# Hybrid attention and SSD backbone on one core: low passes of the value product one key block later, the context rows' norm in nine steps, a modulation with one pass less

## The chip, the cores and the metric

The kernel runs on one core of one Trainium2 chip. The metric is the device time of one execution in microseconds (us). TensorE is called PE, its weight loads PEld, VectorE DVE, ScalarE ACT, GpSimd POOL, and SyncE, which issues most transfers, SP. Each engine works through its own instructions in a fixed order and waits for the others by semaphores. The transfers that an engine issues stand in that same order.

## The reference

The kernel computes a two-layer network for 1024 latent rows and 256 context rows with a model width of 1024. Layer 0 is windowed attention (16 query heads, 4 key heads, blocks of 128 rows; each block sees its neighbours and the context), layer 1 a bidirectional state-space mixer (SSD). The parts that the change touches are these:

```python
for i in range(DEPTH):
    shift, scale, gate = adaln(c, w_ada[i], b_ada[i])          # likewise *_c for the context
    u = rms_normalize(h) * (1.0 + scale[:, None]) + shift[:, None]
    uc = rms_normalize(hc) * (1.0 + scale_c) + shift_c
    y, yc = attention_mixer(u, uc, ...) if i % 2 == 0 else ssd_mixer(u, uc, ...)
    h = h + gate[:, None] * y
    if i < DEPTH - 1:
        hc = hc + gate_c * yc

# in attention_mixer, for a block of queries
s = jnp.einsum('bqkgd,bskd->bkgqs', qb, kb).astype(jnp.float32) * scale
p = sink_softmax(s, sink_kg, mask).astype(vb.dtype)
o = jnp.einsum('bkgqs,bskd->bqkgd', p, vb)
y_lat = ((o * jax.nn.silu(g)) @ w_out).astype(h_lat.dtype)
```

## The kernel before

**Numbers in two halves.** A float32 operand is split into a high part (a cast on ACT) and a low part (operand minus high part), and a product is three passes on PE: high by high, low by high, high by low (L236 to L238 for the projections). The names ending in H and L, or h and l, are these parts: `uH` and `uL` of the normed rows, `wh` and `wl` of the weights (L222 cast, L224 subtraction on POOL), `ph` and `pl` of the transposed softmax weights.

**Tiles.** The rows are held in three tiles, 0 and 1 with 512 latent rows each and 2 with the 256 context rows, transposed, so that a tile is eight slabs of 128 columns of the model by its rows. A norm (`rstd_n`, from L357) sums squares over partitions with PE (L354), takes the root on ACT and POOL (L362, L363), builds a diagonal on DVE (L365), spreads it over the partitions with PE (L367), and copies it on ACT (L369). `modulate` (L290) then makes the two parts of u for one slab: a product with the norm on DVE (L297), scale and shift on ACT (L298), a copy on ACT as the high part (L299), and a subtraction on DVE as the low part (L300). `xc` is the context's input. It runs for tile 1 and the context near the start, and again for each of the three tiles between the layers.

**Attention.** A unit is one block of 128 queries with one key head; 40 units run in the order context, tile 0, tile 1. `att_front` makes a unit's scores (L645, L646, which read the queries from `qs` and `qz`) and its softmax (L649 and after, on DVE and ACT). `att_back` runs one unit later: for each key block four transposes on PE (L670), the cast `ph` on ACT (L674), the subtraction `pl` on DVE (L675), then the high pass (L676) and the low pass (L677) of the value product into the bank `pv`. After the last block two transposes of `rs` (L683) and the output's steps follow. `qz` has two buffers whose unused halves are zeroed once (L711).

**Filling.** Between key blocks `tick` calls `advance`, which puts parts of other projections into PE's order, so that PE has work while the softmax is made: during the units of the context and of tile 0 the gates and queries of tile 1 (`qg1`; `gq` and `qf` are buffers of its results), during the units of tile 1 the output projection of the context and then of tile 0 (`out_steps`). `total` is the number of parts, and parts are spread evenly over the key blocks by it. An output projection has eight row groups (`one`), each in PARTS = 8 parts. Before a group's parts stands the load of its weights, and h is read by SP (L732), updated (L736) and written back (L737). When the eight groups of a tile are done, `fin` runs as a single step: the norm, and for each of the eight slabs a reload of h by SP (L756, two `h1` buffers) and `modulate`. The context's `fin` so stands as one step between the context's projection and tile 0's.

**Order.** A list scheduler works out each engine's order in advance, from its own estimate of times; `high_priority` and `issue_after` in `advance` say where a part may go. An edit in one place can move instructions in others.

## Time and profile before

| what | value |
|---|---|
| median of 3 runs | 1836.33 us (1835.45 to 1843.21) |
| the profiled execution | 1840.92 us |
| its span in the profile | 1839.2 us |
| granted TensorE clock, mean | 0.988 |
| bytes moved | 227.62 MB, 124 GB/s mean |

The span runs from the first to the last instruction of the profiled execution. A row of a timeline reads: start, duration, engine, line, operation, output and inputs with their shapes, how many instructions; in brackets the idle time of the engine just before, and what ended it. A row of waits reads: the engine and its instruction, the one it waited for, then total, count and longest. A window reads: its length, and the busy time of PE, PEld, DVE, ACT and POOL in it with their instructions. A busy share says nothing by itself of what holds the program up; for that one looks where PE, the engine with the most work, is not busy, and at what it waits for there.

### The profile page before, as it was taken

What the parts mean: (1) busy time and instruction counts of PE and PEld (TensorE: products, weight loads), DVE (VectorE), ACT (ScalarE), POOL (GpSimd) and SP (SyncE); (2) the same over time, 40 slices, a digit from 0 to 9 for tenths busy, and PEclk for the clock granted to TensorE, in tenths of its full rate; (3) what the DMA queues carried; (4) which work ended last, traced back from release to release, by engine and by line L of the source; (5) the groups of instructions that cost most, each with busy time, mean ns of one, the idle gap of its engine ahead of it and who ended that gap; (6) DMA issues with size and microseconds to landing.
All of it is one profiled execution on the core that took longest, in us unless ns stands there. A gap on an engine that the chain in (4) does not pass through costs nothing. (4 is left out here: it accounts for less than half of the span.)

```text
span 1839.2 us, 29059 instructions
## 1 busy us (share of the span) xinstructions
PE 1757.5 (96%) x10319; PEld 1503.1 (82%) x10319; DVE 1171.9 (64%) x2136; ACT 893.0 (49%) x1956; POOL 803.2 (44%) x1066
## 2 busy tenths in 40 slices
PE   6899999999999999899999999999999999999997
PEld 2697778888888787678889898988989898888886
DVE  4544426778887765674766757676675767675643
ACT  3722227777777765562443535344353434454422
POOL 1331116555566454102454554545455454554321
PEclk8999999999999999999999999999999999999998
DMA  8648855544455445321323323232232324456542
GB/s 303 241 127 263 284 179 141 121 97 107 112 130 130 109 129 187 99 70 41 87 69 78 93 66 83 76 92 67 80 93 64 86 73 101 148 165 171 180 138 69
DMA packets 212497, 227.62 MB, mean 124 GB/s; under 512 B 16384, under 2 KB 149632, under 8 KB 212352
## 3 DMA queue, kind: packets, MB, share of 16 engines
q1 hardware_dynamic: 178288, 207.12, 37.8%
q0 software_dynamic: 34064, 18.65, 5.6%
q8 instruction: 81, 1.33, 0.3%
q14 instruction: 64, 0.52, 0.1%
HBM read 190.88 MB, written 35.13 MB: 123 GB/s over the span
## 5 line engine op out<-in xcount | busy, mean ns | idle before, releaser
L236 PE MATMUL pj<-uH,wh 128*128 128x512 f32 (+1 forms) x712 | 256.4, 362 | 11.3 <-ACT uH L457 8.3
L238 PE MATMUL pj<-uH,wl 128*128 128x512 f32 (+1 forms) x712 | 243.7, 343 | 1.2 <-POOL wl L224 1.2
L237 PE MATMUL pj<-uL,wh 128*128 128x512 f32 (+1 forms) x712 | 244.2, 343 | 0.4 <-DVE uL L458 0.4
L1157 POOL TENSOR_TENSOR xw<-xn,dtdec 128x256 f32<-128x256 f32 x144 | 107.6, 750 | 199.5 <-PE psD L1182 127.1
L224 POOL TENSOR_TENSOR wl<-wr,wh 128x512 fp32r<-128x512 f32 x92 | 121.6, 1325 | 117.6 <-ACT wh L222 114.1
L1088 PE MATMUL pj<-uH,wh 128*128 128x512 f32 x512 | 165.9, 400 | 3.6 <-ACT bn L1042 2.2
L236 PEld LDWEIGHTS pj<-uH,wh 128*128 128x128 f32 x712 | 135.8, 191 | 39.2 <-ACT uH L457 9.6
L1088 PE MATMUL pj<-uL,wh 128*128 128x512 f32 x512 | 167.4, 400 | 0.2 <-DVE uL L300 0.2
L1088 PE MATMUL pj<-uH,wl 128*128 128x512 f32 x512 | 166.9, 400 | 0.7 <-DVE wl L1019 0.7
L1113 PE MATMUL pj<-wh,uH 128*128 128x256 f32 x512 | 151.7, 296 | 2.6 <-ACT xn L1042 2.6
L675 DVE TENSOR_TENSOR pl<-pt,ph 128x512 fp32r<-128x512 f32 x168 | 114.5, 687 | 58.2 <-ACT ph L674 57.0
L238 PEld LDWEIGHTS pj<-uH,wl 128*128 128x128 f32 x712 | 135.5, 190 | 18.4 <-POOL wl L224 2.1
L1113 PE MATMUL pj<-wh,uL 128*128 128x256 f32 x512 | 149.8, 293 | 0.0
L237 PEld LDWEIGHTS pj<-uL,wh 128*128 128x128 f32 x712 | 136.0, 191 | 16.9 <-issue 3.1
L1113 PE MATMUL pj<-wl,uH 128*128 128x256 f32 x512 | 147.1, 287 | 0.0
L222 ACT CAST wh<-wr 128x512 fp32r<-128x512 f32 (+1 forms) x132 | 84.7, 645 | 105.7 <-PE pj L237 82.2
L649 DVE CUSTOM_DVE_ANT_0 sm<-S,mask,nsink 128x640 f32<-128x640 f32 (+2 forms) x160 | 119.3, 771 | 22.0 <-PE S L646 14.7
L674 ACT CAST ph<-pt 128x512 fp32r<-128x512 f32 x168 | 97.6, 586 | 59.4 <-PE pt L670 55.6
L651 ACT ACTIVATE sm<-sm,nm 128x640 f32<-128x640 f32 (+2 forms) x160 | 118.7, 743 | 14.7 <-DVE nm L649 14.2
L1088 PEld LDWEIGHTS pj<-uH,wh 128*128 128x128 f32 x512 | 94.6, 189 | 23.8 <-ACT xn L1042 2.4
L1088 PEld LDWEIGHTS pj<-uL,wh 128*128 128x128 f32 x512 | 96.7, 189 | 20.6 <-DVE uL L300 0.5
L1088 PEld LDWEIGHTS pj<-uH,wl 128*128 128x128 f32 x512 | 96.4, 189 | 20.4 <-DVE wl L1019 1.1
(372 smaller groups left out, 4811.3 us busy)
## 6 DMA issues: line engine op xcount, KB each, us to landing
wr<-w_x SPq DMA_DIRECT2D x32, 512.0 KB, 3.9
M<-acs SPq DMA_DIRECT2D x64, 256.0 KB, 5.3
bw<-acs SPq DMA_DIRECT2D x64, 256.0 KB, 5.0
wr<-wo SPq DMA_DIRECT2D x48, 256.0 KB, 2.7
wr<-w_sk SPq DMA_DIRECT2D x24, 512.0 KB, 4.0
wr<-wg SPq DMA_DIRECT2D x40, 256.0 KB, 4.8
qs<-q POOLq DMA_DIRECT2D x40, 256.0 KB, 3.9
wada<-w_ada SPq DMA_DIRECT2D x16, 512.0 KB, 6.7
```

The source lines that it names most:

```text
L222: nc.scalar.copy(h, raw)
L224: (eng or nc.vector).tensor_tensor(l, raw, h, op=ALU.subtract)
L236: self.nc.tensor.matmul(ps, lh, rh, start=first and i == 0, stop=False)
L237: self.nc.tensor.matmul(ps, lh, rl, start=False, stop=False)
L238: self.nc.tensor.matmul(ps, ll, rh, start=False, stop=last and i == n - 1)
L649: nc.vector.tensor_tensor_reduce(out=sm[:, :W], in0=Sv, in1=self.mask[:, m0 : m0 + W], scale=-SCALE, scalar=self.nsink[:, 4 * j + r : 4 * ...
L651: nc.scalar.activation(sm[:, :W], sm[:, :W], AF.Exp, bias=nm[:, r : r + 1], scale=-1.0, accum_out=sums[:, r : r + 1])
L674: nc.scalar.copy(ph, ptf)
L675: nc.vector.tensor_sub(pl, ptf, ph)
L1088: nc.tensor.matmul(raw[:, 512 * i : 512 * i + 512], l[:, k, :], r[i][:, k, :], start=k + y == 0, stop=k == KT - 1 and y == 2)
L1113: nc.tensor.matmul(pj[:, c], l, r[:, k, :], start=c % 2 + q + k + y == 0, stop=c % 2 == 1 and q == 1 and k == 3 and y == 2)
L1157: nc.gpsimd.tensor_tensor(xw, X(st, c).rearrange("p (r h) -> p r h", r=R), self.dtdec[:, c, hd(d, g)].unsqueeze(2).broadcast_to([P, R, HP] ...
```

## The change

Four edits go together.

1. `modulate` has one ACT pass less: DVE multiplies by scale and norm in one step, ACT adds the shift and writes the high part, DVE adds the shift again and takes the high part off.
2. In `att_back` the low pass of a key block is issued behind the transposes, cast and subtraction of the next block, ahead of that block's high pass; the last one follows the transposes of `rs`.
3. The context's `fin` is gone. Its norm and its eight modulations are nine steps in the list `side`. One of them is taken after every SIDE = 6 parts of tile 0's output projection. The context's projection is cut into CPARTS = 4 parts for a group instead of 8, so `total` is 97 parts instead of 130. The norm is kept in a buffer of the name `ut`. Tile 0's and tile 1's `fin` stay.
4. The zeros of `qz` are written by POOL instead of DVE.

```diff
--- before.py
+++ after.py
@@ -49,6 +49,8 @@
 AHEAD = 1
 PACE = 4
 PARTS = 8
+CPARTS = 4
+SIDE = 6
 SLACK = (0, 0, 0)
 QC = 5
 FIRST = 5
@@ -294,10 +296,9 @@
         m = self.mod[layer]
         sc, sh = m[:, 8 + k, c : c + 1], m[:, k, c : c + 1]
         uh, ul = self.uH[i][:, k, :], self.uL[i][:, k, :]
-        nc.vector.tensor_mul(h, h, r)
-        nc.scalar.activation(h, h, AF.Identity, bias=sh, scale=sc)
-        nc.scalar.copy(uh, h)
-        nc.vector.tensor_sub(ul, h, uh)
+        nc.vector.scalar_tensor_tensor(h, in0=h, scalar=sc, in1=r, op0=ALU.mult, op1=ALU.mult)
+        nc.scalar.activation(uh, h, AF.Identity, bias=sh)
+        nc.vector.scalar_tensor_tensor(ul, in0=h, scalar=sh, in1=uh, op0=ALU.add, op1=ALU.subtract)
 
 
     def xin(self, i):
@@ -664,6 +665,12 @@
         ps = self.psA
         j, b, i, o, kb, sms, sg, rs = st
         pv = t(ps, [P, 512], F32, "pv")
+        lows = []
+
+        def low(last=False):
+            bb, pl = lows.pop(0)
+            return nc.tensor.matmul(pv, self.v[:, bb, j, :], pl, start=False, stop=last)
+
         for x, bb in enumerate(kb):
             pt = t(ps, [P, R, P], F32, "pt")
             for r in range(R):
@@ -673,14 +680,17 @@
             ptf = pt.rearrange("p r n -> p (r n)")
             nc.scalar.copy(ph, ptf)
             nc.vector.tensor_sub(pl, ptf, ph)
-            nc.tensor.matmul(pv, self.v[:, bb, j, :], ph, start=x == 0, stop=False)
-            mm = nc.tensor.matmul(pv, self.v[:, bb, j, :], pl, start=False, stop=x == len(kb) - 1)
+            if x:
+                low()
+            mm = nc.tensor.matmul(pv, self.v[:, bb, j, :], ph, start=x == 0, stop=False)
+            lows.append((bb, pl))
             self.last.append(mm.ins)
             tick()
 
         pt = t(ps, [P, 512], F32, "pt")
         for e in range(2):
             nc.tensor.transpose(pt[:, e * P : (e + 1) * P], rs[:, e].rearrange("p x d -> p (x d)"), self.ident)
+        low(True)
         nc.vector.tensor_mul(sg, sg, pt[:, : 2 * P].rearrange("p (a n) -> p a n", a=2))
         co = t(self.pb, [HD, 512], F32, "co")
         nc.scalar.copy(co, pv[HD:, :])
@@ -708,7 +718,7 @@
         oH, oL = [None] * 3, [None] * 3
         self.qz = [t(p, [P, R, P], F32R, f"qz{z}") for z in range(2)]
         for z in range(2):
-            nc.vector.memset(self.qz[z][(1 - z) * HD : (2 - z) * HD].bitcast(F32), 0.0)
+            nc.gpsimd.memset(self.qz[z][(1 - z) * HD : (2 - z) * HD].bitcast(F32), 0.0)
 
         def qg1(src, out, x):
             w = self.load_halves(a[src][x], nc.gpsimd)
@@ -731,7 +741,7 @@
                     st[m] = h1
                 nc.sync.dma_start(h1, self.xin(i)[m * P : (m + 1) * P, :])
                 out = []
-                yield from self.proj_g(out, ps, w, oH, oL, i, "S" if i == 1 and m % 3 else "pj", parts=1 if i == 1 else PARTS)
+                yield from self.proj_g(out, ps, w, oH, oL, i, "S" if i == 1 and m % 3 else "pj", parts={0: PARTS, 1: 1, 2: CPARTS}[i])
                 pj = out[0]
                 nc.vector.scalar_tensor_tensor(h1, in0=pj[:, :n], scalar=self.mod[0][:, 16 + m, c : c + 1], in1=h1, op0=ALU.mult, op1=ALU.add)
                 nc.sync.dma_start(self.h_d[m][i], h1)
@@ -743,24 +753,33 @@
                     nc.scalar.activation(sq, h1, AF.Square)
                     (nc.vector if i == 1 else nc.gpsimd).tensor_tensor(st["acc"], st["acc"], sq, op=ALU.add)
 
+            def norm():
+                p = self.po
+                rout = (p, [P, n], F32, "ut" if i == 2 else "sqa")
+                st["r"] = self.rstd_c(p, st["acc"], n, D, rout=rout, dout=(p, [P, 512], F32, "dg0"))
+                self.alloc_u(i)
+
+            def mod(k):
+                if i == 1:
+                    h = st[k]
+                else:
+                    h = t(self.po, [P, n], F32, "h1")
+                    nc.sync.dma_start(h, self.h_d[k][i])
+                self.modulate(1, h, st["r"], i, k)
+
             def fin():
                 yield
-                p = self.po
-                r = self.rstd_c(p, st["acc"], n, D, rout=(p, [P, n], F32, "sqa"), dout=(p, [P, 512], F32, "dg0"))
-                self.alloc_u(i)
-                for k in range(KT):
-                    if i == 1:
-                        h = st[k]
-                    else:
-                        h = t(p, [P, n], F32, "h1")
-                        nc.sync.dma_start(h, self.h_d[k][i])
-                    self.modulate(1, h, r, i, k)
-
-            return [lambda m=m: one(m) for m in range(KT)] + [fin]
+                for f in steps:
+                    f()
+
+            steps = [norm] + [lambda k=k: mod(k) for k in range(KT)]
+            if i == 2:
+                self.side = steps
+            return [lambda m=m: one(m) for m in range(KT)] + ([] if i == 2 else [fin])
 
         pr = [lambda x=x: qg1("wg", self.g_out, x) for x in range(8)] + [lambda x=x: qg1("wq", self.q_out, x) for x in range(8)]
         fill = {2: pr[:QC], 0: pr[QC:], 1: out_steps(2) + out_steps(0)}
-        total = {2: QC * PARTS, 0: (16 - QC) * PARTS, 1: 16 * PARTS + 2}
+        total = {2: QC * PARTS, 0: (16 - QC) * PARTS, 1: KT * (CPARTS + PARTS) + 1}
         units = [(i, j, b) for i, blocks in ((2, range(8, 10)), (0, range(0, 4)), (1, range(4, 8))) for b in blocks for j in range(KV)]
         nkb = lambda b: 2 if b >= 8 else 2 + min(b + 2, 8) - max(b - 1, 0)
         count = {i: sum(nkb(u[2]) for u in units if u[0] == i) - SLACK[i] for i in range(3)}
@@ -788,6 +807,8 @@
                 if next(cur, "end") == "end":
                     cur = None
             done[i] += 1
+            if i == 1 and self.side and done[i] > KT * CPARTS and (done[i] - KT * CPARTS) % SIDE == 0:
+                self.side.pop(0)()
 
         pend = [self.att_front(p, x, *units[x]) for x in range(AHEAD)]
         for _ in range(FIRST):
@@ -807,6 +828,7 @@
                 pend.append(self.att_front(p, x + AHEAD, *units[x + AHEAD]))
             self.att_back(p, pend.pop(0), oH, oL, tick)
         tick(True)
+        assert not self.side
         ckv.close()
         self.cf = ExitStack()
         self.pf = self.pool("front", ctx=self.cf, side="right")
```

How the instructions stand in each engine's order now is shown at three places. The first is DVE near the start, where tile 1 and the context are normed; L297 and L300 are the modulation, L365 the context's diagonal, L512 to L515 the rotation of keys, and `gq` is a gate that frees a result bank for PE. Before:

```order
L512 TENSOR_TENSOR qf_206_716<-pj_205_691,cos_167_488 128x512
L513 STREAM_SHUFFLE rope_b_208_718<-pj_205_691 128x512
L300 TENSOR_TENSOR uL1_181_589<-uH2_165_484,uH1_180_588 128x512 x2
L515 TENSOR_TENSOR qf_206_716<-qf_206_716,rope_b_208_718 128x512
L300 TENSOR_TENSOR uL1_181_589<-uL2_166_485,uH1_180_588 128x512 x3
L297 TENSOR_TENSOR xc_61_160<-xc_61_160,rr512_186_632 128x256 x4
L297 TENSOR_TENSOR xc_62_161<-xc_62_161,rr512_186_632 128x256 x4
L300 TENSOR_TENSOR uL1_181_589<-uL2_166_485,uH1_180_588 128x512
L553 TENSOR_SCALAR gq_174_570<-gq_174_570,pj_104_249 128x512
L300 TENSOR_TENSOR uL2_188_635<-xc_61_160,uH2_187_634 128x256 x4
```

Now (L299 and L301 are the modulation's steps, L366 the diagonal):

```order
L301 TENSOR_SCALAR uL1_181_589<-uH2_165_484,mod0_5_74,uH1_180_588 128x512 x4
L366 TENSOR_TENSOR sqt_184_620<-ident_1_63,rc_183_617 128x256
L301 TENSOR_SCALAR uL1_181_589<-uL2_166_485,mod0_5_74,uH1_180_588 128x512 x4
L513 TENSOR_TENSOR qf_206_700<-pj_205_675,cos_167_488 128x512
L514 STREAM_SHUFFLE rope_b_208_702<-pj_205_675 128x512
L299 TENSOR_SCALAR xc_61_160<-xc_61_160,mod0_5_74,rr512_186_624 128x256 x4
L299 TENSOR_SCALAR xc_62_161<-xc_62_161,mod0_5_74,rr512_186_624 128x256 x4
L554 TENSOR_SCALAR gq_174_570<-gq_174_570,pj_104_249 128x512
L301 TENSOR_SCALAR uL2_188_627<-xc_61_160,mod0_5_74,uH2_187_626 128x256
L516 TENSOR_TENSOR qf_206_700<-qf_206_700,rope_b_208_702 128x512
```

The low parts of tile 1 now stand together ahead of the context's steps; `gq` follows those eight directly, and the sum of the rotation (L515, now L516) comes behind it.

The second is PE in the middle of attention, at one unit's first key block: a score (L646, now L647), the high pass (L676, now L685), the low pass (L677, now L672), four transposes of the third block (L670, now L677), and projection passes (L236 to L238, now L238 to L240). Before:

```order
L646 MATMUL S_826_3662<-kL1_195_678,qz1_490_2535 128x256
L676 MATMUL pv_798_3566<-ph_800_3572,v_193_676 128x512
L677 MATMUL pv_798_3566<-pl_801_3573,v_193_676 128x512
L670 MATMUL pt_805_3595<-ident_1_63,sm_746_3389 128x128
L670 MATMUL pt_805_3595<-ident_1_63,sm_748_3397 128x128
L670 MATMUL pt_805_3595<-ident_1_63,sm_750_3405 128x128
L670 MATMUL pt_805_3595<-ident_1_63,sm_752_3413 128x128
L676 MATMUL pv_798_3566<-ph_803_3586,v_193_676 128x512
L236 MATMUL pj_815_3625<-uH1_180_588,wh_766_3449 128x512
L237 MATMUL pj_815_3625<-uL1_181_589,wh_766_3449 128x512
L238 MATMUL pj_815_3625<-uH1_180_588,wl_767_3451 128x512
```

Now, at the unit that follows:

```order
L647 MATMUL S_856_3761<-kL0_194_661,qz0_489_2518 128x256
L685 MATMUL pv_836_3685<-ph_838_3691,v_193_660 128x512
L238 MATMUL pj_815_3608<-uH1_180_588,wh_769_3438 128x512
L239 MATMUL pj_815_3608<-uL1_181_589,wh_769_3438 128x512
L240 MATMUL pj_815_3608<-uH1_180_588,wl_770_3440 128x512
L672 MATMUL pv_836_3685<-pl_839_3692,v_193_660 128x512
L677 MATMUL pt_843_3713<-ident_1_63,sm_789_3516 128x128
L677 MATMUL pt_843_3713<-ident_1_63,sm_791_3524 128x128
L677 MATMUL pt_843_3713<-ident_1_63,sm_793_3532 128x128
L677 MATMUL pt_843_3713<-ident_1_63,sm_795_3540 128x128
L685 MATMUL pv_836_3685<-ph_841_3704,v_193_660 128x512
```

The low pass stood directly behind the high pass, and now has three projection passes ahead of it; the second block's transposes stand ahead of the scores in both. Over the whole program the two passes stand directly together 98 times of 168 before and 17 times now.

The third is DVE at the context's second norm: its diagonal (L365, now L366), the modulation steps (L297 and L300, now L299 and L301) among softmax steps (L649, now L650) and low parts of the softmax weights (L675, now L682). Before:

```order
L675 TENSOR_TENSOR pl_1693_6896<-pt_1691_6890,ph_1692_6895 128x512
L675 TENSOR_TENSOR pl_1697_6918<-pt_1695_6912,ph_1696_6917 128x512
L365 TENSOR_TENSOR dg0_1706_6941<-ident_1_63,rc_1705_6938 128x256
L297 TENSOR_TENSOR h1_1711_6949<-h1_1711_6949,sqa_1708_6945 128x256
L297 TENSOR_TENSOR h1_1712_6955<-h1_1712_6955,sqa_1708_6945 128x256
L649 ISA sm_1684_6862,nm_1674_6827<-S_1683_6857,mask_196_679,nsink_197_680 128x640
L649 ISA nm_1674_6827 128x1
L649 ISA sm_1741_7070,nm_1737_7059<-S_1740_7065,mask_196_679,nsink_197_680 128x640
L649 ISA nm_1737_7059 128x1
L675 TENSOR_TENSOR pl_1721_7003<-pt_1719_6997,ph_1720_7002 128x512
L675 TENSOR_TENSOR pl_1732_7035<-pt_1730_7029,ph_1731_7034 128x512
L300 TENSOR_TENSOR uL2_1710_6948<-h1_1711_6949,uH2_1709_6947 128x256
```

Now:

```order
L694 TENSOR_TENSOR sgt_1571_6436<-sgt_1571_6436,pt_1659_6762 128x256
L299 TENSOR_SCALAR h1_1698_6899<-h1_1698_6899,mod1_6_75,ut_1653_6744 128x256
L682 TENSOR_TENSOR pl_1658_6754<-pt_1656_6748,ph_1657_6753 128x512
L650 ISA sm_1669_6795,nm_1663_6776<-S_1668_6790,mask_196_663,nsink_197_664 128x640
L650 ISA nm_1663_6776 128x1
L659 RECIPROCAL sums_1616_6613<-sums_1616_6613 128x4
L301 TENSOR_SCALAR uL2_1655_6747<-h1_1698_6899,mod1_6_75,uH2_1654_6746 128x256
L650 ISA sm_1671_6803,nm_1663_6776<-S_1670_6798,mask_196_663,nsink_197_664 128x640
L650 ISA nm_1663_6776 128x1
L682 TENSOR_TENSOR pl_1679_6828<-pt_1677_6822,ph_1678_6827 128x512
L699 TENSOR_TENSOR ot_1661_6769<-pv_1628_6657,co_1660_6767 64x256 x2
```

Two products stood directly behind the diagonal, and the eight modulations followed within the next units; now one modulation stands among the steps of a unit, and the next comes 22 rows later. On PE, 14 matmuls stood between the norm's row sums and its broadcast, and five do now; at tile 0's norm it was thirteen, and is six.

## The prediction

> **What bounds the kernel now.** I read the page's busy shares first, then the waits of PE (total, count, longest).
>
> ```profile
> span 1839.2 us, 29059 instructions
> PE 1757.5 (96%) x10319; PEld 1503.1 (82%) x10319; DVE 1171.9 (64%) x2136; ACT 893.0 (49%) x1956; POOL 803.2 (44%) x1066
> ...
> PE pv L677 <- DVE pl L675: 7.6, 17, 1.7
> PE pj L236 <- DVE gq L553: 3.6, 1, 3.6
> PE S L646 <- DVE qz L711: 1.8, 1, 1.8
> ```
>
> TensorE is busy for 1757.5 of 1839.2 us, so a rearrangement can free at most the other 81.7, and what is lost where the granted clock is low. The change leaves TensorE as many matmuls as before. It pays, or costs, only through waits of PE and the clock; the last three rows are waits on lines that it touches. Two places hold more than such a wait, and windows show them (busy time of PE, PEld, DVE, ACT, POOL; clock; DMA share; GB/s).
>
> ```profile
> 88.00:92.00 4.00, 0.45 (x2) 0.45 (x3) 4.00 (x11) 4.00 (x10) 0.00 (x0) 0.75 0.09 32
> 92.00:96.00 4.00, 4.00 (x21) 4.00 (x21) 3.23 (x10) 3.27 (x10) 1.42 (x3) 0.50 0.28 74
> 96.00:100.00 4.00, 4.00 (x19) 3.48 (x19) 1.14 (x4) 0.37 (x1) 1.43 (x3) 0.89 0.96 198
> ...
> 600.00:630.00 30.00, 26.44 (x135) 20.09 (x136) 26.43 (x63) 25.84 (x61) 11.43 (x20) 0.94 0.36 92
> 620.00:630.00 10.00, 8.21 (x40) 6.76 (x40) 8.39 (x20) 7.56 (x19) 2.97 (x6) 0.83 0.27 81
> 630.00:710.00 80.00, 79.75 (x432) 66.47 (x431) 41.27 (x89) 46.20 (x102) 44.85 (x55) 1.00 0.43 127
> ```
>
> From 88 us PE stands still while DVE and ACT are full: these are the first norms, of tile 1 and the context. From 600 to 630 us PE loses 3.56 us and 0.06 of its clock, with DVE at 88% and ACT at 86%: that is the context rows' second norm. The 80 us behind it hold the same attention work and lose a quarter of a microsecond. So in that stage it is the norm that costs.
>
> **The change part by part.**
>
> *1. First norms with the lighter modulation.* PE waits for gq, and gq waits for DVE's order: all of this stands ahead of it.
>
> ```profile
> 72.96 2.67 DVE L297 TENSOR_TENSOR uH<-uH,rr 128x512 f32<-128x512 f32 x4 [1.89 <-ACT rr L369]
> 75.55 2.49 DVE L297 TENSOR_TENSOR uL<-uL,rr 128x512 f32<-128x512 f32 x4
> 79.36 0.43 DVE L365 TENSOR_TENSOR sqt<-ident,rc 128x256 f32<-128x256 f32 x1 [0.72 <-POOL rc L363]
> 81.02 0.74 DVE L513 STREAM_SHUFFLE rope_b<-pj 128x512 f32<-128x512 f32 x1
> 82.96 1.17 DVE L300 TENSOR_TENSOR uL<-uH,uH 128x512 fp32r<-128x512 f32 x1 [0.53 <-ACT uH L299]
> 87.54 2.76 DVE L297 TENSOR_TENSOR xc<-xc,rr 128x256 f32<-128x256 f32 x8
> 90.22 0.68 DVE L300 TENSOR_TENSOR uL<-uL,uH 128x512 fp32r<-128x512 f32 x1
> 90.83 0.67 DVE L553 SCALAR_TENSOR_TENSOR gq<-gq,pj 128x512 f32<-128x512 f32 x1
> 91.55 0.58 PE L236 MATMUL pj<-wh,uH 128*128 128x256 f32 x1 [3.58 <-DVE gq L553]
> ```
>
> DVE's steps stay as many. The form with a scalar, which now replaces the plain one, costs the same: 0.67 (gq) against 0.68. What falls is ACT, two passes to one, so DVE no longer idles for copies (the 0.53 at 82.96), and in the new order gq stands right behind the eight xc steps, ahead of the rope sum. From start to start four of the first steps take 2.59 us (72.96 to 75.55) and one low part 0.61 (90.22 to 90.83). From 72.96 the new chain is then eight first steps (5.2 us), eight low parts (4.9), the diagonal (0.43), two rope steps (1.3), xc (2.76) and gq (0.67), about 15.2 us. Gq then ends near 88.2 instead of 91.50, and PE resumes 3.3 us earlier. The half clock comes with the still stretch; it costs 2.0 us in 92 to 96 (half of 4), 0.44 in 96 to 100 (0.11 of 4) and 0.2 of the 0.45 us that PE worked ahead: 2.65. Sum **+6.0 us**. Low end +0.9 (only the idle time of 0.53 and some of a step go, the clock falls as before); high end +6.2 (the whole 3.58 and 2.65).
>
> *2. The qz memset moves from DVE to POOL.*
>
> ```profile
> 269.47 0.69 DVE L553 SCALAR_TENSOR_TENSOR qf<-qf,pj 128x512 f32<-128x512 f32 x1 [5.27 <-ACT qf L552]
> 270.97 0.48 DVE L711 MEMSET qz<- 64x512 f32 x1 [0.16 <-issue]
> 270.86 0.50 PE L646 MATMUL S<-kL,qz 128*128 128x256 f32 x2 [1.82 <-DVE qz L711]
> ```
>
> DVE idles for 5.27 us, then does qf and last the memsets, so the scores stand for 1.82 us. On POOL the memsets can lie under that idle time; qf and what follows it are still waited for. **+1.2 us**, between 0 (something else is as late) and 1.8.
>
> *3. The context's second norm in nine steps.* In the pile at 600 to 630 us no projection matmul runs between the first two rows here, because the weights of tile 0's first rows stand behind the eight reloads on SP.
>
> ```profile
> 604.84 0.40 PE L238 MATMUL pj<-uH,wl 128*128 128x512 f32 x1
> 629.35 0.50 PE L236 MATMUL pj<-uH,wh 128*128 128x512 f32 x1
> 610.73 8.71 SPq L756 DMA_DIRECT2D h<-h  x3
> 621.13 0.43 DVE L297 TENSOR_TENSOR h<-h,sqa 128x256 f32<-128x256 f32 x1 [2.04 <-DMA h<-h]
> 622.21 0.57 PE L677 MATMUL pv<-pl,v 128*128 128x512 f32 x1 [1.66 <-DVE pl L675]
> PEld pv L677 <- DVE pl L675: 4.8, 7, 2.0
> PEld S L645 <- DVE nm L649: 2.0, 6, 0.8
> ```
>
> By the window the loss is 3.56 us of PE and 0.06 × 30 = 1.8 of clock: 5.4. By the weight loads' waits from 598 to 630 us it is 6.8 and the clock: 8.6. I take 7.0, the middle, since a weight load's wait may lie beside a running matmul. Spread out, a step is one reload, two DVE steps of 0.43 us and one ACT pass, once in six parts of tile 0's projection. DVE is 52% busy from 630 to 710 (41.27 of 80), which hides them; without that cover each costs its 0.9 us, 7 us in all, and the gain is gone. New is a wait for the norm itself:
>
> ```profile
> 594.84 0.48 PE L236 MATMUL pj<-uH,wh 128*128 128x512 f32 x1
> 595.35 0.72 POOL L363 TENSOR_TENSOR rc<-rc,half 128x2 f32<-128x2 f32 x1 [1.45 <-ACT rc L362]
> 596.11 0.97 DVE L365 TENSOR_TENSOR dg<-ident,rc 128x256 f32<-128x256 f32 x1 [1.75 <-POOL rc L363]
> 598.15 0.59 PE L367 MATMUL pt<-dg,ones 128*128 128x256 f32 x2
> ```
>
> From the end of the row sums (594.84) to the diagonal (596.11 + 0.97 = 597.08) pass 2.24 us. Between them and the broadcast PE had 14 matmuls, 3.31 us or 0.236 each; now it has five, 1.18 us. Behind the wait stand the transposes of the next block. That is 1.1 us, and I put 1.4, as a weight subtraction on POOL can lie ahead. Net **+5.6 us**; low 0 or less (a rival, below), high 8.6 − 1.1 = 7.5.
>
> *4. Low passes one block later.* Waits for pl are 7.6 us, of which the windowed view puts 2.5 between 598 and 630, in step 3; 5.1 remain. High and low stand directly together 98 times of 168 in PE's order before, 17 after. But only 17 low passes waited at all, mostly at a unit's first block, where DVE has the next unit's softmax steps and the last one's output ahead of pl. There the new order only moves three matmuls from between the blocks to between high and low; the same transposes and scores lie ahead of the low pass, so DVE is as late as it was. **+1.0 us**; at best all 5.1; at worst −3 (40 units whose last low pass, now behind the two transposes of rs, delays the output copy by less than 0.1 us each).
>
> *5. Lighter modulation at tiles 0 and 1.*
>
> ```profile
> L299 ACT CAST uH<-h1k x8: 602/608/614, 771.5 to 781.7; 128x512 fp32r<-128x512 f32 x8
> 743.18 1.76 DVE L300 TENSOR_TENSOR uL<-h,uH 128x512 fp32r<-128x512 f32 x1
> 742.69 1.70 POOL L224 TENSOR_TENSOR wl<-wr,wh 128x512 fp32r<-128x512 f32 x1 [3.78 <-ACT wh L222]
> ```
>
> Eight copies of 0.61 us, 4.9 in all, leave ACT's chain at tile 1, which PE follows closely; a third of it, +1.5, I count. Tile 0's row sums now have six matmuls ahead of the broadcast instead of thirteen; by step 3's chain that is a wait of 2.24 − 6 × 0.236 = 0.8, with POOL's queue 1.0 the other way. **+0.5 us**, between −1 and +3.
>
> *6. Layer 1.* Its first groups are ordered anew; no work is added. **0**, ± 3.4 us, two stretches of low clock as here (0.28 × 6 = 1.7):
>
> ```profile
> 844.00:850.00 6.00, 6.00 (x36) 5.95 (x37) 3.71 (x5) 1.03 (x1) 1.97 (x4) 0.72 0.17 65
> ```
>
> The sum is 6.0 + 1.2 + 5.6 + 1.0 + 0.5 + 0 = 14.3 us, 0.78%. The profiled execution took 1840.92 us (the span and 1.7 around it), 4.6 above the median of 1836.33 and inside the runs' 1835.45 to 1843.21. Against itself that makes 1826.6, against the median **1822.0 us**.
>
> The clock fell to 0.50 behind the wait of 3.58 us, and to 0.83 over 620 to 630, where the longest wait I found is 1.66. The Trainium skill (TensorE: Matmul & The Clock Gate, The HAM clock gate) has the clock halved after a whole idle window of about 3.4 us. The first row agrees, the second does not. By that rule step 3 would not win back its 1.8 us, and the sum would be 12.5.
>
> **The rivals.**
>
> *The spread norm gives back what it frees.* For it: its 16 DVE steps now lie in a stretch where PE loses nothing (79.75 of 80), so each pl that they delay is new. The row at 743.18 took 1.76 us instead of 0.68 beside a weight subtraction on POOL at 742.69. Against: DVE is half idle there. Seven steps' worth, 0.9 each plus half a microsecond in some, cancels step 3: 14.3 − 5.6 = 8.7, 1827.6 us. The Trainium skill (SBUF — State Buffer, Who interferes with whom) says that a VectorE instruction with two SBUF inputs and a GpSimd one lock each other out; the two rows agree with that.
>
> *The reloads stop DVE.* DVE works in order, so a modulation that waits for its reload holds the pl behind it, as at 621.13 (2.04 us), with PE's 1.66 at 622.21. If every one does, and each time the clock loses 1.8 more: 8 × 3.46 = 27.7 against the 14.3 + 1.4 of all else, 12 us slower, 1848 us. It decides from 15.7 / 3.46 = 4.5 of the eight on. For: the reload is issued in the same step as the modulation, on the queue of the weights. Against: it lands soon, as the issues of h in 590 to 630 show, and DVE has other steps ahead.
>
> ```profile
> DMA to landing us min/median/max: 1.9/2.4/3.7
> ```
>
> *The low pass pays in full,* 5.1 instead of 1.0: 1818 us. For: 17 waits by name. Against: DVE's order in step 4.
>
> *It does not do what it says:* PE may wait as long for the context's u as for gq; step 1 is then +0.9 and the time 1827.1, as in the first rival.
>
> **How the numbers follow.** The sum has a chance of 0.55, the give-back (with the last) 0.20, the stopped DVE 0.13, the full low pass 0.12. Half a percent, 9.2 us, is about what a measurement of this kernel can tell from no change: faster means below 1827.1. Of the sum 0.50 lies below and 0.05 within; the full low pass lies below (0.12); of the give-back 0.06 lies below, 0.13 within, 0.01 beyond; of the stopped DVE 0.12 is slower and 0.01 within. That makes faster 0.68, same 0.19, slower 0.13. Downwards the range takes all upper bounds together, 0.2 + 0.6 + 1.9 + 4.1 + 2.5 + 3.4 = 12.7, 1809, as none of them is hard. Upwards it takes the give-back, 1827.6, with step 1 at its low end (5.1 more) and layer 1 on the wrong side: 1836.
>
> **What would show it.** Step 1: PE's wait for gq under 1 us, and a full clock from 88 to 96. Step 2: no wait for qz. Step 3: no 20 us without projection matmuls, PE over 98% where 600 to 630 stood, about 1 us of wait ahead of the norm's broadcast. Step 4: waits for pl of some 4 us outside it. Wrong would be new waits of PE for pl or nm during tile 0's projection, each behind a DVE that waits for a DMA, or a clock that falls elsewhere.

## The result and the profile after

The changed kernel takes 1831.37 us (median of 20 runs, 1825.9 to 1836.27) beside 1837.30 us of the kernel before (20 runs, 1831.35 to 1844.62). The ratio is 0.9964, with an interval of 0.9952 to 0.9976: 0.36% faster, which is 6.6 us (the two medians differ by 5.9), where 14.3 us were forecast. The time lies inside the predicted range, and the gain is less than half of the forecast. All ratios below are to runs of the kernel before on the same chip. The profiled execution took 1834.43 us, with a span of 1832.7.

First the busy row of the page after and PE's longest waits on the lines that the change touches (total, count, longest):

```profile
PE 1750.5 (96%) x10319; PEld 1500.3 (82%) x10319; DVE 1172.5 (64%) x2134; ACT 875.7 (48%) x1916; POOL 805.7 (44%) x1068
...
PE S L647 <- DVE nm L650: 3.5, 3, 1.8
PE pv L685 <- DVE ot L699: 2.4, 5, 1.3
PE pj L238 <- DVE rope_b L514: 2.3, 1, 2.3
PE pj L238 <- ACT uH L702: 2.3, 1, 2.3
PE pv L685 <- ACT ph L681: 2.1, 5, 0.7
PE pt L368 <- DVE dg L366: 1.6, 2, 1.0
PE pj L238 <- DVE v L589: 1.6, 1, 1.6
PE pv L672 <- DVE pl L682: 1.6, 5, 0.5
```

None of the three waits of the prediction's first fence is left: those for gq and qz are gone, that for pl fell from 7.6 to 1.6 us. Yet the list is as long as it was. Scores wait for nm, the high pass for ph and for ot (the step that reads the bank pv), a projection for rope_b, v and the last output uH. PE's busy time fell by 7.0 us and the span by 6.5, so PE idles as long as before, 82.2 us instead of 81.7. Next, windows of the changed kernel at the places of the prediction (busy PE, PEld, DVE, ACT, POOL; clock; DMA share; GB/s):

```profile
84.00:88.00 4.00, 1.66 (x10) 1.46 (x9) 4.00 (x8) 0.51 (x1) 1.23 (x1) 0.87 0.00 0
88.00:92.00 4.00, 3.88 (x24) 3.68 (x23) 4.00 (x10) 2.91 (x7) 0.20 (x1) 0.70 0.00 0
92.00:96.00 4.00, 2.63 (x23) 2.43 (x21) 4.00 (x10) 1.81 (x5) 1.09 (x2) 1.00 0.53 142
...
600.00:630.00 30.00, 29.49 (x166) 24.74 (x165) 23.56 (x53) 22.16 (x50) 16.09 (x24) 1.00 0.40 110
630.00:710.00 80.00, 76.73 (x431) 64.01 (x430) 52.62 (x114) 51.85 (x116) 40.79 (x56) 1.00 0.42 116
```

The pile at 600 to 630 us is gone (0.51 us lost instead of 3.56, full clock). But the 80 us behind it now lose 3.27 instead of 0.25. At the first norms PE stands earlier: from 84 to 88 us it is busy for 1.66 us. The kernel before had 3.09 there:

```profile
84.00:88.00 4.00, 3.09 (x24) 2.69 (x22) 4.00 (x7) 2.81 (x7) 1.82 (x1) 1.00 0.09 34
```

DVE is as full as it was.

Single profiles have to be read with care here. To compare several, I cut PE's work at equal points (each matmul counted with the lower quartile of the steps of its form in the kernel before) and took the time between them. The table gives these stretches in us for the kernels that are told of below, but for the two under "Two prices on DVE".

| kernel | start | first norms | attention begins | attention | context norm, tile 0's projection | tile 0's norm | from there into layer 1 |
|---|---|---|---|---|---|---|---|
| before | 53.3 | 47.9 | 45.7 | 280.8 | 134.0 | 59.2 | 208.8 |
| only memset | 51.1 | 47.4 | 45.7 | 281.5 | 133.5 | 58.5 | 209.7 |
| only parts | 51.0 | 47.4 | 48.0 | 277.6 | 132.5 | 57.9 | 210.0 |
| only norm | 47.8 | 47.2 | 45.7 | 277.9 | 132.4 | 56.8 | 208.2 |
| only low passes | 46.2 | 47.2 | 47.5 | 279.8 | 134.7 | 60.7 | 206.2 |
| only modulation | 51.4 | 47.1 | 45.7 | 281.5 | 136.0 | 58.6 | 202.5 |
| changed | 53.3 | 47.1 | 47.5 | 279.9 | 131.9 | 60.7 | 200.7 |
| changed, again | 46.0 | 47.1 | 46.6 | 280.4 | 131.2 | 62.0 | 201.9 |
| last low pass earlier | 48.4 | 47.1 | 47.6 | 280.5 | 131.4 | 60.4 | 202.1 |
| late passes only at the end | 51.4 | 47.1 | 47.6 | 280.1 | 130.8 | 60.0 | 200.4 |
| at once at the end | 46.0 | 47.1 | 46.7 | 280.0 | 133.2 | 57.7 | 202.0 |
| no late passes | 46.1 | 47.1 | 47.3 | 278.0 | 129.1 | 50.8 | 204.4 |
| no late passes, reload ahead | 46.2 | 47.1 | 48.3 | 278.2 | 129.2 | 52.5 | 203.4 |

The start is the same code with the same order on PE everywhere and varies between 46 and 53 us, so a difference of that size between two profiles' totals says nothing of the change. The rows from "changed" to "late passes only at the end" are four executions of one and the same order: in their traces every engine has the same instructions in the same sequence, also where the code was edited (more of this below). They still differ by up to 2.0 us in the other stretches. Only what several rows share counts below.

### The profile page after: what moved, and what is told of

Read it like the earlier page. It is cut to its first block, busy times and chain, and to the rows that moved or that the text cites. A ratio compares the mean times of both kernels' runs of the same rounds, so it can differ in the third digit from the quotient of the medians.

```text
span 1832.7 us, 28996 instructions
## 1 busy us (share of the span) xinstructions
PE 1750.5 (96%) x10319; PEld 1500.3 (82%) x10319; DVE 1172.5 (64%) x2134; ACT 875.7 (48%) x1916; POOL 805.7 (44%) x1068
## 5 line engine op out<-in xcount | busy, mean ns | idle before, releaser
L238 PE MATMUL pj<-uH,wh 128*128 128x512 f32 (+1 forms) x712 | 251.5, 355 | 17.5 <-ACT uH L458 8.3
L240 PE MATMUL pj<-uH,wl 128*128 128x512 f32 (+1 forms) x712 | 244.6, 344 | 0.7 <-POOL wl L226 0.7
L1179 POOL TENSOR_TENSOR xw<-xn,dtdec 128x256 f32<-128x256 f32 x144 | 103.6, 722 | 189.8 <-PE psD L1204 113.0
L238 PEld LDWEIGHTS pj<-uH,wh 128*128 128x128 f32 x712 | 136.6, 192 | 46.3 <-ACT wh L224 10.3
L240 PEld LDWEIGHTS pj<-uH,wl 128*128 128x128 f32 x712 | 136.4, 192 | 18.2 <-POOL wl L226 1.1
L682 DVE TENSOR_TENSOR pl<-pt,ph 128x512 fp32r<-128x512 f32 x168 | 114.0, 688 | 55.6 <-ACT ph L681 54.2
L650 DVE CUSTOM_DVE_ANT_0 sm<-S,mask,nsink 128x640 f32<-128x640 f32 (+2 forms) x160 | 119.5, 772 | 34.5 <-PE S L647 20.7
L681 ACT CAST ph<-pt 128x512 fp32r<-128x512 f32 x168 | 96.8, 584 | 49.8 <-PE pt L677 47.9
```

Source lines behind the costliest of these rows:

```text
L238: self.nc.tensor.matmul(ps, lh, rh, start=first and i == 0, stop=False)
L240: self.nc.tensor.matmul(ps, ll, rh, start=False, stop=last and i == n - 1)
L650: nc.vector.tensor_tensor_reduce(out=sm[:, :W], in0=Sv, in1=self.mask[:, m0 : m0 + W], scale=-SCALE, scalar=self.nsink[:, 4 * j + r : 4 * ...
L681: nc.scalar.copy(ph, ptf)
L682: nc.vector.tensor_sub(pl, ptf, ph)
L1179: nc.gpsimd.tensor_tensor(xw, X(st, c).rearrange("p (r h) -> p r h", r=R), self.dtdec[:, c, hd(d, g)].unsqueeze(2).broadcast_to([P, R, HP] ...
```

## The experiments

**One edit at a time.** Four kernels were made of the kernel before, each with one part of the change.

```diff
# e1_mod_only: the three new lines of modulate
# e2_low_only: the new att_back
# e3_norm_only: CPARTS, SIDE and the list of steps, old modulate, old att_back
# e4_memset_only
-            nc.vector.memset(self.qz[z][(1 - z) * HD : (2 - z) * HD].bitcast(F32), 0.0)
+            nc.gpsimd.memset(self.qz[z][(1 - z) * HD : (2 - z) * HD].bitcast(F32), 0.0)
```

> Only the lighter modulation, all else as before. Theory A (a DVE step that reads a scalar from memory per partition costs 0.06 us more than the plain product, and the rope step that frees PE's result bank now stands behind the low parts): PE's wait near 88 us is replaced by waits of about 2.3 us for the rope step and some for others, the first norms gain at most 1 us, and whatever is gained comes between 740 and 850 us, 0 to 5 us there. Time 0 to 6 us below before. Rival (the prediction's step 1): gq ends 3 us earlier, PE's wait for it is under 1 us, the clock stays full from 88 to 96, and the first norms alone give about 6 us.

Measured: 0.9982 of before (0.9966 to 0.9998), 3.3 us. Theory A holds. The first norms take 47.1 us instead of 47.2 to 47.9 in the five kernels with the old modulation, a gain of 0.1 to 0.8; the rest lies behind attention, 202.5 us in the last column instead of 206 to 210, of which the stretch with the context's norm takes some back (136.0 instead of 133.5 to 134.0). PE's waits near 90 us, in this kernel's list of waits:

```profile
PE pj L236 <- DVE rope_b L512: 2.3, 1, 2.3
PE pj L236 <- DVE v L587: 1.6, 1, 1.6
PE pj L236 <- DVE gq L552: 0.2, 1, 0.2
```

> Only the low passes one block later. Theory A (the stall moves, since DVE and ACT set the pace there and the bank pv is released later): PE's waits for pl fall from 7.6 to under 2.5 us, and waits of the high pass (for ph, or for the step that releases pv) and of the scores for nm grow by about as much; time within 2 us of before. Rival 1 (the prediction's): the waits for pl stay at 4 us or more. Rival 2: the waits for pl go and nothing takes their place, 5 us faster.

Measured: 1.0007 (0.9991 to 1.0023), no change that can be told. Theory A holds: the stall moves.

```profile
PE pv L684 <- DVE ot L698: 1.9, 6, 0.5
PE pv L684 <- ACT ph L680: 1.7, 4, 0.7
PE pv L671 <- DVE pl L681: 1.6, 4, 1.0
```

Waits for pl fell from 7.6 to 1.6 us; waits of the high pass for ot rose from nothing to 1.9, and two for nm took 2.4.

> Only the context's norm in nine steps with four parts a row group (old modulation, old low passes, memset on DVE). Theory A: the pile near 600 to 630 us goes (6 to 8 us), a wait of about 1 us ahead of the broadcast comes, and without the later release of pv tile 0's projection loses under 2 us more than before: 4 to 6 us faster. Rival (the spread norm gives back what it frees by itself): new waits of 4 us or more from 630 to 710 us also here, time within 2 us of before.

Measured: 0.9978 (0.9963 to 0.9994), 4.0 us. The time fits theory A. But the rival is true in part as well: late in tile 0's projection, from 650 to 670 us, PE loses 3.5 us and the clock falls. DVE's timeline there follows two windows of this kernel:

```profile
650.00:660.00 10.00, 8.56 (x51) 7.13 (x52) 8.44 (x19) 7.22 (x17) 5.45 (x8) 1.00 0.59 149
660.00:670.00 10.00, 7.91 (x40) 6.46 (x39) 5.92 (x15) 5.63 (x14) 2.89 (x5) 0.83 0.39 80
```

```profile
657.19 1.29 DVE L677 TENSOR_TENSOR pl<-pt,ph 128x512 fp32r<-128x512 f32 x2
662.42 0.43 DVE L299 TENSOR_TENSOR h<-h,ut 128x256 f32<-128x256 f32 x1 [3.94 <-DMA h<-h]
662.76 0.68 DVE L677 TENSOR_TENSOR pl<-pt,ph 128x512 fp32r<-128x512 f32 x1
```

A modulation waited 3.94 us for its reload with a pl behind it, and the low pass stood for 2.1 us: the rival of the stopped DVE, in one of eight steps.

> Only qz's zeros on POOL instead of DVE. Theory A (the second softmax step near 272 us waits for something that comes at the same time anyway): PE's wait for qz goes and a wait for nm of 1.3 to 1.9 us takes its place; time within 1 us of before, or up to 2.5 us slower where the clock falls at 272 to 280 us. Rival (the prediction's step 2): 1.2 us faster, no new wait there.

Measured: 1.0002 (0.9986 to 1.0018). Theory A holds, with 1.8 us of waiting for nm in place of 1.8 for qz; the stretch is 45.7 us in both. The softmax step that these scores wait for could not have come sooner. The changed kernel's timeline shows it waiting for a store, and the same row of e4 has the same 1.83 us:

```profile
269.92 0.48 DVE L650 CUSTOM_DVE_ANT_0 sm<-S,mask,nsink 128x256 f32<-128x256 f32 x1
270.32 0.08 DVE L650 DVE_READ_ACCUMULATOR2_ANT nm<- 128x1 f32 x1
272.23 0.48 DVE L650 CUSTOM_DVE_ANT_0 sm<-S,mask,nsink 128x256 f32<-128x256 f32 x1 [1.83 <-DMA sg<-qf]
```

**The late passes taken out of the change.** Next, the changed kernel without them, with the last one of a unit put earlier, and with the reloads ahead; and the parts of the norm's edit alone.

```diff
# e5_no_low: the changed kernel with the old att_back
# e6_last_low: the changed kernel
-            nc.tensor.transpose(pt[:, e * P : (e + 1) * P], rs[:, e].rearrange("p x d -> p (x d)"), self.ident)
-        low(True)
+            ...
+        low(True) ahead of this loop
# e7_reload_ahead: e5, and in mod(k) of the context
+                if i == 2 and k + 1 < KT:
+                    load(k + 1)
# e8_parts_only: the kernel before
-parts=1 if i == 1 else PARTS
+parts={0: PARTS, 1: 1, 2: CPARTS}[i]
```

> The changed kernel with the old place of the low passes. Theory A (the later low pass costs by itself, some 2 us at the end of attention where the last output waits for it, and its waits are paid elsewhere): PE's wait for the attention output near 717 us falls from 2.3 us to 0.5, waits for pl come back, and the time is 2 to 4 us below the changed kernel, 0.993 to 0.995 of before. Rival (the prediction's step 4): 1 us slower than the changed kernel, 0.997 of before.

Measured: 1820.96 us, 0.9912 of before (0.9890 to 0.9933), far below what either theory expected. Without its late passes the change gains 16 us instead of 6.6. The wait for the output (uH) fell to 0.4 us as theory A says, and tile 0's norm takes 50.8 us instead of 60 to 62, a gain that theory A had put at 2.

> The changed kernel with only the last low pass of a unit ahead of the two transposes of rs. Theory A (bank pv and the output come late because of that last pass): the waits of the high pass for the step that releases pv (2.4 us) and of the output projection (2.3 us) fall to a third, time 1 to 3 us below the changed kernel. Rival (it is the next units' softmax on DVE that releases pv late): these waits stay, the same time within 1 us.

Measured: 0.9959 (0.9944 to 0.9973), as the changed kernel; the waits for ot (2.4 us) and uH (2.3 us) are the same to the tenth. This decides nothing between the two theories, though. The planner (the list scheduler) gave the edited lines the order that it had given the unedited ones: in the two traces all five engines have the same instructions in the same sequence. The run is the changed kernel once more, and as such of use: beside it, on the same chip, the kernel without late passes took 10.4 us less (1820.96 against 1831.33 us).

> As the previous but one (old low passes), and each reload of the context's h is issued one step ahead into buffers of its own (square buffers two instead of three). Theory A (DVE stands for reloads, 7.2 us in the changed kernel, and the pl behind is late): DVE's waits for these reloads fall under 1 us, PE's stalls between 600 and 700 us fall by 2 to 4 us, and so does the time against the kernel without the reload ahead. Rival (the steps are what costs, not their reloads): DVE's waits fall, PE's stalls stay.

Measured: 0.9914 (0.9899 to 0.9929), the same as without the reload ahead. DVE's waits for the context's reloads fell to 0.9 us, as theory A says. PE's stalls stayed (the stretch with the context's norm takes 129.2 us and 129.1 without the reload ahead), and the time did not fall. So the rival holds by the numbers, but the edit did more than it was meant to: the planner now has the eight modulations between 585 and 606 us, where they were spread from 583 to 659. This kernel also has one square buffer less, which can hide a gain. What the run does show is that without late passes the time is low a second time, with tile 0's norm at 52.5 us.

> The kernel before with four parts a row group in the context's projection (98 parts instead of 130), its norm still one step. Theory A (the nine steps make the gain, the parts only the pace): the pile with its loss of 6 us or more stays where the context's norm runs, time within 1.5 us of before. Rival (the evener filling makes the gain): 3 us or more faster, PE's waits for pl before the norm a third fewer.

Measured: 0.9985 (0.9969 to 1.0000), 2.8 us, nearer to the rival. Attention alone takes 277.6 us instead of 281, as in the kernel with the whole norm edit (277.9), and the stretch with the context's norm 132.5 us, as there (132.4). So what can be told of that edit's gain belongs to the evener filling. That the nine steps add anything by themselves is not shown: the two kernels differ by 0.0007 in time, far inside either interval.

**Two prices on DVE.**

```diff
# e9_constants: the changed kernel
-        nc.vector.scalar_tensor_tensor(h, in0=h, scalar=sc, in1=r, op0=ALU.mult, op1=ALU.mult)
+        nc.vector.scalar_tensor_tensor(h, in0=h, scalar=1.0, in1=r, op0=ALU.mult, op1=ALU.mult)
-        nc.vector.scalar_tensor_tensor(ul, in0=h, scalar=sh, in1=uh, op0=ALU.add, op1=ALU.subtract)
+        nc.vector.scalar_tensor_tensor(ul, in0=h, scalar=0.0, in1=uh, op0=ALU.add, op1=ALU.subtract)
# e10_rope_on_dve: the changed kernel
-        nc.gpsimd.tensor_tensor(b, b, self.sin[:, s : s + n], op=ALU.mult)
+        (nc.vector if i == 0 else nc.gpsimd).tensor_tensor(b, b, self.sin[:, s : s + n], op=ALU.mult)
```

> The changed kernel with constants 1 and 0 in place of scale and shift in the two DVE steps of the modulation; it leaves out the scale and the low part's shift. Theory A (reading a scalar per partition from memory costs 0.06 us a step): the 128x512 steps of the first norms take 0.68 us instead of 0.74 and the 128x256 ones 0.41 instead of 0.47, from start to start 0.60 and 0.335; gq ends about 1.5 to 1.9 us earlier after the first of them. Rival (the form itself is dearer): they stay at 0.74 and 0.47.

> The changed kernel with tile 0's rope product on DVE instead of POOL. Theory A (a DVE step that reads two operands from memory stands still while POOL does a product of its own): the longest of the eight xc steps at the first norms falls from 1.50 us to 0.47, and the eight together from 4.26 to about 3.2; the step beside POOL's weight subtraction near 81 us stays at 1.7 to 1.8. Rival (the long xc step waits for its data): it stays at 1.5.

The product steps of the first norms, by tile (min/median/max in ns), in the changed kernel, with constants, and with the rope product on DVE:

```profile
L299 DVE SCALAR_TENSOR_TENSOR xc<-xc,mod,rr x8: 467/473/1497, 86.6 to 90.4; 128x256 f32<-128x256 f32 x8
L299 DVE SCALAR_TENSOR_TENSOR uL<-uL,mod,rr x4: 742/742/745, 76.0 to 78.0; 128x512 f32<-128x512 f32 x4
```

```profile
L299 DVE SCALAR_TENSOR_TENSOR xc<-xc,rr x8: 400/410/1512, 84.0 to 87.5; 128x256 f32<-128x256 f32 x8
L299 DVE SCALAR_TENSOR_TENSOR uL<-uL,rr x4: 676/678/679, 73.5 to 75.3; 128x512 f32<-128x512 f32 x4
```

```profile
L299 DVE SCALAR_TENSOR_TENSOR xc<-xc,mod,rr x8: 462/472/472, 79.3 to 82.1; 128x256 f32<-128x256 f32 x8
```

With constants the medians are 0.41 and 0.68 us instead of 0.47 and 0.74: the scalar from memory costs 0.06 us a step, at both widths. The chain to the end of gq became only 0.6 us shorter, though, not 1.5 to 1.9, because the diagonal took 1.50 us instead of 0.42 beside POOL's weight subtraction, after a wait of 0.59 (the longest xc step is still 1.51). The product that holds that xc step in the changed kernel is this one, and DVE's long step lies beside it:

```profile
86.77 1.42 POOL L515 TENSOR_TENSOR rope_b<-rope_b,sin 128x512 f32<-128x512 f32 x1 [3.87 <-DVE rope_b L514]
```

With the rope product on DVE the long step is gone, 1.50 to 0.47, and the eight take 3.23 us instead of 4.26. So the price of the scalar and the reason of the long step are as theory A has them in both; the gain on gq's chain is not. In both kernels, where the changed kernel has 47.1, the first norms take 46.0 and 46.1 us. There was one run of each, 1837.89 and 1825.69 us, which says little by itself.

**Where the late passes cost.**

```diff
# e11_low_at_once_at_end: the changed kernel, in the loop over key blocks
-            if x:
+            if lows:
                 low()
...
             lows.append((bb, pl))
+            if b == 7:
+                low(x == len(kb) - 1)
# e12_late_only_at_end: the same with
+            if not (i == 1 and b == 7):
# e13_changed_same_chip: the changed kernel itself
```

> The changed kernel with the low pass at once behind the high pass in the four units of the last block, and one block later everywhere else. Theory A (the loss at the end of attention comes from these units' late passes): the stretch around tile 0's norm loses 8 to 10 us less, as without the later low passes, and the time is 6 to 9 us below the changed kernel. Rival 1 (the order that the planner finds for the row sums and the projections there, which stays as it was: six matmuls ahead of the broadcast, none between the transposes of rs and the product that needs their output): that stretch loses as much as in the changed kernel, time within 2 us of it. Rival 2 (only the output's wait is theirs): 2 us.

> The reverse of the kernel before: the low passes one block later only in the four units of the last block, at once behind the high pass everywhere else. Theory A (it is the late passes of the last units that cost): as slow as the changed kernel on the same chip, 0.995 to 0.997 of before. Rival 1 (the late passes of all other units cost, through the waits of high passes and scores that replace those for pl): as fast as without late passes, 0.990 to 0.993. Rival 2 (each costs half): 0.993 to 0.995.

> The changed kernel itself beside the kernel with late passes only at the end, on one chip with the same runs of before. Theory: 0.995 to 0.9975 as measured, so that the other differs from it by 0 (theory A), by 0.4 to 0.5 percent (rival 1) or by a quarter percent (rival 2). Its profile also gives a second execution of the changed kernel: stretches whose length differs by over 1 us from the first (the start, the clock near 275 us, the start of layer 1) are chance, and equal ones belong to the kernel.

Measured: e11 0.9906 (0.9883 to 0.9929), e12 0.9971 (0.9956 to 0.9987), e13 0.9966 (0.9953 to 0.9979). Read by the times alone, theory A would hold in both. The traces say otherwise. e12 has the order of the changed kernel on all five engines, instruction for instruction: issuing the low pass at once in 36 of the 40 units moved nothing. In e11 PE's order differs from the changed kernel's in 7 of 10319 places, all in the last units. So e12 is one more measurement of the changed kernel, e11 nearly one, and that the last four units are to blame is not shown.

What moves the order is another line of the same edit. `self.last` is a list of markers: for each key block it keeps the matmul behind which `advance` may put filling parts. In the kernel before and in e5 that is the low pass; in the changed kernel, e6, e11 and e12 it is the high pass, because `mm` now names that one. The filling parts go in front of the low pass: 616 projection matmuls stand between a high pass and its low pass in the changed kernel's order on PE, 220 before and 198 in e5. e11 and e12 between them issue every unit's low pass at once and keep the new order, so the marker is what is left as its cause; no run moves the marker alone.

What the new order costs shows at the end of attention. Here are the first 55 us from just before tile 0's norm, in e12 (the changed kernel's order), e11 and e5:

```profile
702.00:757.00 55.00, 47.37 (x210) 36.47 (x208) 32.71 (x43) 21.85 (x38) 20.97 (x15) 0.97 0.56 183
```

```profile
699.00:754.00 55.00, 50.14 (x220) 39.32 (x219) 35.21 (x45) 22.85 (x39) 20.05 (x16) 0.94 0.60 192
```

```profile
690.00:745.00 55.00, 52.35 (x240) 41.24 (x239) 34.17 (x46) 23.61 (x40) 22.72 (x17) 1.00 0.63 200
```

PE is busy for 47.4, 50.1 and 52.4 of the 55 us, with 210, 220 and 240 matmuls; the changed kernel's second profile has 47.3. From e12 to e5 that is 5.0 us of standing and, with the clock at 0.97 and 1.00, 1.7 us of clock, 6.6 of the 10 us. Part of it is seen in PE's timeline behind tile 0's row sums, first in the changed kernel, then without late passes:

```profile
713.75 1.10 PE L368 MATMUL pt<-dg,ones 128*128 128x512 f32 x2 [0.63 <-DVE dg L366]
714.68 0.38 PE L692 MATMUL pt<-ident,rs 128*128 128x128 f32 x2
717.36 0.50 PE L238 MATMUL pj<-uH,wh 128*128 128x512 f32 x1 [2.29 <-ACT uH L702]
```

```profile
699.47 0.38 PE L684 MATMUL pt<-ident,rs 128*128 128x128 f32 x2
699.61 0.49 PE L238 MATMUL S<-uH,wh 128*128 128x512 f32 x1
...
702.15 0.50 PE L238 MATMUL pj<-uH,wh 128*128 128x512 f32 x1 [0.39 <-ACT uH L693]
```

Without late passes ten projection matmuls stand between the row sums and the broadcast, and six more in front of the product that needs the last output. In the changed order it is six and none, and PE stands for 0.63 and 2.29 us, after which the clock falls. The waits for weights and for h1k are a further part: 4.4 us in the changed kernel's list for this stretch, 1.0 in e5's.

e11 stays open. It has the two waits of 0.63 and 2.29 us, too; what it lacks is most of those for weights and h1k, since on SP a load of weights now stands ahead of one of h1k. Its times are as good as without late passes, but the changed kernel was not run on its chip, where single runs of e9 and e10, with the changed kernel's order in attention, came to 0.998 and 0.991 of before. Its profile, without the start, is as long as the changed kernel's: 1779.9 us against 1779.4 and 1781.8, and 1767.9 in e5.

## Why the prediction was wrong, step by step

The direction was right, the size was not: 6.6 us instead of 14.3. Two terms of the sum failed above all, step 4 and step 1.

**Step 4** was put at "+1.0 us; at best all 5.1; at worst −3". In the changed kernel its edit costs 0.0052 of the time, about 9.6 us (0.9964 against 0.9912), and 10.4 us between the medians on one chip (e6 against e5). "There the new order only moves three matmuls from between the blocks to between high and low" was a true reading of the order, and it was taken to be harmless. The argument looked at what these matmuls do inside a unit and missed that they are the stock that fills the end of attention, where PE then stands. By itself the edit costs next to nothing (e2, 1.0007): the 9.6 us are lost only beside the other edits. A second statement fell as well: "DVE is as late as it was" was taken to keep the waits for pl, but they went, from 7.6 to 1.6 us, and others came in their place.

**Step 1**, +6.0, came to 0.3 us (47.1 against a mean of 47.4 in the kernels with the old modulation; 0.8 against the one profile of before). Three parts of it were wrong. "The form with a scalar ... costs the same: 0.67 (gq) against 0.68": gq's scalar is a constant, and the modulation's lies in memory, 0.74 and 0.47 us. Gq was taken to be PE's only wait. In the new order all low parts stand ahead of the rope step that frees PE's bank, so PE waits for rope_b from 84.4 to 86.75 us, where the forecast let it run on as before:

```profile
81.68 3.77 DVE L301 SCALAR_TENSOR_TENSOR uL<-uL,mod,uH 128x512 fp32r<-128x512 f32 x4
85.98 0.72 DVE L514 STREAM_SHUFFLE rope_b<-pj 128x512 f32<-128x512 f32 x1
86.75 0.41 PE L238 MATMUL pj<-wh,uH 128*128 128x256 f32 x1 [2.34 <-DVE rope_b L514]
86.59 4.26 DVE L299 SCALAR_TENSOR_TENSOR xc<-xc,mod,rr 128x256 f32<-128x256 f32 x8
90.78 0.67 DVE L554 SCALAR_TENSOR_TENSOR gq<-gq,pj 128x512 f32<-128x512 f32 x1
```

From the first step at 73.27 to the end of gq at 91.45 it is 18.2 us instead of the 15.2 forecast: the eight xc steps took 4.26 us instead of 2.76, the low parts beside POOL's subtraction 3.77 instead of 2.5. And the 2.65 us for the clock were worth nothing here. In the changed kernel's first profile the clock fell at this place (0.87 and 0.70 from 84 to 92 us). In its second, where all comes 7.3 us earlier, it did not:

```profile
76.70:80.70 4.00, 1.66 (x14) 1.46 (x13) 4.00 (x8) 0.51 (x1) 1.22 (x1) 1.00 0.00 0
80.70:84.70 4.00, 2.37 (x20) 2.16 (x20) 4.00 (x10) 2.91 (x7) 0.22 (x1) 1.00 0.00 0
```

The first norms took 47.1 us in both. What shortened them was a shorter chain on DVE (46.0 and 46.1 us in e9 and e10). The low end of the step, +0.9, was near.

**Step 2**, +1.2, came to nothing; its low end named the reason, something else as late.

**Step 3**, +5.6, came near in size, 4.0 us alone (e3, 1.1 to 6.8 by the interval), but by another way, which is luck. The forecast has the gain where the context's norm runs. Of e3's gain some 3 us lie in attention (277.9 instead of 280.8 us) and 1.1 to 1.6 in the stretch with the norm, and the evener parts bring both without the nine steps (e8); the forecast gave the parts nothing. The new wait ahead of the broadcast was forecast as 1.1 to 1.4 us and measured as

```profile
588.37 0.67 PE L368 MATMUL pt<-dg,ones 128*128 128x256 f32 x2 [0.99 <-DVE dg L366]
```

The rival that gives back what is freed was right to a good part: where the pile stood 3.0 us less are lost, and from 630 to 710 us 3.0 us more. Beside the light modulation and without late passes that stretch takes 129 us (e5 and e7) instead of 132, so together they do help.

**Steps 5 and 6**, +0.5, were too small. The modulation alone gives 3.3 us, and the kernels of the table that have it take 200 to 204.4 us in the last column against 206 to 210. The kernel with constants, in its one run, took 207.3 there, and layer 1's start also depends on the clock, so the size is not sure. Step 5's new wait at tile 0's norm, forecast as 0.8 to 1.0 us, is the 0.63 named above.

Step 1 brought 5.7 us less than forecast, step 2 1.2 less, step 3 1.6 less and step 4 some 10 less; steps 5 and 6 brought more. The forecast added up its terms, and the edits don't add up: three of them alone give 0.9982, 0.9978 and 1.0002, a product of 0.9962, 7 us, but together, without late passes, 0.9912, 16 us. The low passes' edit then takes back nearly all that the three have in common. The forecast had neither of the two, and that its sum came out with the right sign although step 4 lost so much is owed to the first. Most of the joint gain shows at tile 0's norm (50.8 us against 56.8 to 58.6 with one edit), where several short waits for weights and outputs go only when DVE, ACT and PE's filling are all eased; that this is the reason is argued, not shown.

The best version is therefore the change without its late passes, 1820.96 us (0.9912 of before).

## What to carry to other kernels

A wait that a list names is not its price: where the engine behind it is the pace, removing the wait moves it to the next row, and only the stretch's length tells. Matmuls that fill gaps are a stock; an edit that uses them earlier can be paid at the end of the stage, so look at what fills the last chain of a stage before and after. Where a planner makes the order, compare the executed orders before reading an experiment: e6 and e12 moved lines of code and not one instruction. And take the price of an instruction from a row with the same kind of operands, not only the same form.

## What the runs showed of the hardware

- A scalar read from memory per partition cost DVE 0.06 us a step, 0.74 instead of 0.68 us at 128x512 and 0.47 instead of 0.41 at 128x256 (e9).
- A DVE step with two operands in memory stood still while POOL did a product of its own: 1.50 us instead of 0.47, and 0.47 again once that product was moved away (e10). The Trainium skill (SBUF — State Buffer, Who interferes with whom) says that a VectorE instruction with two inputs in SBUF contends with a GpSimd instruction that reads SBUF; these runs agree.
- The same start code took 46 to 53 us from execution to execution, more than the whole change is worth.
- At the beginning of attention the clock fell in some executions and not in others with the same order on PE: 45.7 us without it (before, e1, e3, e4), 47.3 to 48.3 with it (e5, e7, e8; the granted clock from 268 to 272 us was 0.55 in e8 and 1.00 in before). In the changed kernel's first norms it fell in one profile, to 0.87 at 84 to 88 us and 0.70 behind that, and not in another, with the same longest wait of 2.3 us (rope_b). The Trainium skill (TensorE: Matmul & The Clock Gate, The HAM clock gate) has the clock halved after a whole idle window of about 3.4 us; this trace shows no wait of that length there, so the measurement decides.
